# Six gate projections as three pairs of seven block products in a hybrid decoder block on one core

## The chip, the core and the metric

The kernel runs on one core of a Trainium2 chip. A core has a matrix engine (TensorE, PE in the tables, with its weight loads shown as PEld), a vector engine (VectorE, DVE), a scalar engine (ScalarE, ACT), GpSimd (POOL) and a queue that issues transfers (SyncE, SP). Each engine works off its own list of instructions in order and waits where an operand is not there yet. The metric is the device time of one execution in microseconds (us).

## What is computed

One layer of a decoder block over 512 tokens of width 1024, behind 16 learned tokens. Two attention branches, each with a gate, are merged and projected:

```python
u = rmsnorm(h, pre_norm_g[l])
proj = u @ w_in[l]
(..., z_fox, gate_a, gate_b) = jnp.split(proj, split_idx, axis=-1)
y_mla = (o_mla * jax.nn.silu(z_mla)) @ w_br_mla[l]
y_fox = (o_fox * jax.nn.silu(z_fox)) @ w_br_fox[l]
mixed = (jax.nn.sigmoid(gate_a) * y_mla + jax.nn.sigmoid(gate_b) * y_fox) @ w_out[l]
h = h + rmsnorm(mixed, post_norm_g[l])
```

`gate_a` and `gate_b` are u times a 1024x1024 slice of `w_in` each. The kernel computes the sigmoid as a tanh. Branch 0 is the MLA branch (`gate_a`), branch 1 the FoX branch (`gate_b`).

## The kernel before

**Precision.** All large products are of fp32 accuracy out of three reduced ones: every operand is held as a high part and a remainder (h and l), and `hi*hi + hi*lo + lo*hi` is accumulated. A block of weights therefore passes ACT, which writes the high part (`nc.scalar.copy`, L130 or L1052), and then DVE, which subtracts it from the raw weights (`split_lo`, L103). PE starts a product with the high part; its third matmul is the first that needs the remainder.

**A direct unit** (`unit`, L175) makes 128 output features for 512 tokens: 8 contraction blocks times 3 passes, 24 matmuls with 512 columns. `gate_unit` (L526) is such a unit on u, named pg, and ends in a tanh on ACT into a tile th. A `py` unit (L1016) is one on the gated attention output. The list `gates` holds 16 gate units, eight of branch 1 and then eight of branch 0, in the order 0, 4, 1, 5, 2, 6, 3, 7.

**A pair** (`pair_py`, L1063) makes two feature blocks, i and i+4, of the FoX output at once. Tokens, contraction and features are halved, and seven block products (Strassen's scheme in Winograd's form) take the place of eight: each product has 4 contraction blocks times 3 passes, 12 matmuls with 256 columns. They accumulate in three tiles, x, z, y, in the order x, z, x, y, x, z, x. The sums of token blocks S1 to S4 are made once for all four pairs. The sums of weight blocks T1 to T4 are made anew for each pair on DVE (`comb`, L1061), and seven weight blocks are split on ACT and DVE (`take`, L1074). Two raw weight tiles (wraw) hold the blocks b11, b21 and b12, b22.

**Buffers.** The pool wp (L83) holds three raw tiles, three high and three low ones. A load, a cast or a split into one of them waits until its former reader is through.

**Order.** On PE the program's order holds (`manual_schedule`). On the other engines the framework places each instruction when its engine and operands are expected to be free, with the program's order as the priority. Loads go out on SP in the order that this gives.

**The merge stage.** Attention ends at about 402 us. In the order of PE, there follow the last gate units of branch 1 (two of them while the token sums are prepared on DVE), then four times a pair py and two gate units (the last of branch 1, and seven of branch 0), then the eight `py` units of branch 0 with the sixteenth gate unit behind the first of them, then the projection by `w_out`, which uses seven block products too. `halved_g(0)` (L1011) splits the MLA output for the `py` units. `tsum` (L1030) makes the weight sums of the last projection in the tiles tb, one step behind each of the pairs 1 and 2, two behind pair 3. `ssum` (L1037) makes its token sums, behind the `py` units 2, 6 and 7.

Of the kernel before, what the change touches and what calls it, by code (L numbers as in the profile page):

```python
# [11 lines left out]
F32 = mybir.dt.float32  # L12
# [11 lines left out]
S = 512  # L24
# [30 lines left out]
def block_kernel(ctx: ExitStack, tc: tile.TileContext, x, meta_tokens, pre_norm_g, w_in, fox_forget_b,  # L55
# [468 lines left out]
    thx = [None]  # L524

    def gate_unit():  # L526

        i, br = gates.pop(0)

        def done(_, ps):  # L530
            if len(ths) % 7 > 4:
                ths[i, br] = thx[0].tile([128, S], F32, tag="thx", name=f"th{i}{br}")
            else:
                ths[i, br] = thp.tile([128, L], F32, tag="th", name=f"th{i}{br}")[:, 0:S]
            nc.scalar.activation(ths[i, br], ps, AF.Tanh, scale=0.5)
        return unit(f"pg{i}{br}", win_w((O_GA, O_GB)[br], i), u_act, KD, REAL, done)

# [457 lines left out]
    with ExitStack() as mg:  # L995
# [8 lines left out]
        tb = [m1.tile([128, HK, 512], F32, tag=f"tb{n}", name=f"tb{n}") for n in range(4)]  # L1004
# [3 lines left out]
        sh, sl = ([t.rearrange("p k s -> p (k s)")[:, 1024 * j : 1024 * j + 1024].rearrange("p (k s) -> p k s", k=HK)  # L1008
                   for j in range(4)] for t in uT0)

        def halved_g(br):  # L1011
            for k in range(KD):
# [3 lines left out]
        def py(i, br):  # L1016
            def get():
                return by_k(wunit([wbr[br][:, :, 128 * i : 128 * i + 128]])[0], KD)

            def done(_, ps):  # L1020
                nc.vector.scalar_tensor_tensor(out=gT[br][:, i], in0=ths[i, br], scalar=1.0, in1=ps, op0=ALU.add, op1=ALU.mult)
# [29 lines left out]
        def split_to(to, src):  # L1051
            nc.scalar.copy(to[0], src)  # L1052
            split_lo(nc.vector, to[1], src, to[0])
# [6 lines left out]
        def comb(out, p, q, op=ALU.subtract):  # L1060
            nc.vector.tensor_tensor(out=out, in0=p, in1=q, op=op)  # L1061

        def pair_py(i, br):  # L1063

            j, g, wb = i + HK, gT[br], wbr[br]
            ra, rb = (wload([wb[:, :, 128 * f : 128 * f + 128]])[1] for f in (i, j))
            yield
            b11, b21, b12, b22 = ra[:, 0:512], ra[:, 512:], rb[:, 0:512], rb[:, 512:]
            X, Y, Z = (sp.tile([128, 512], F32, tag="s", name=f"{n}{i}{br}")[:, 0:256] for n in "xyz")
            c11, c21, c12, c22 = g[:, i, lo_], g[:, i, up], g[:, j, lo_], g[:, j, up]  # L1070
            th1, th2 = ths[i, br], ths[j, br]
            room = []

            def take(src):  # L1074
# [16 lines left out]
            def gated(dst, th, ts, ps, add):  # L1091
                if add:
                    nc.vector.tensor_tensor(out=dst, in0=ps, in1=dst, op=ALU.add)
                return nc.vector.scalar_tensor_tensor(out=dst, in0=th[:, ts], scalar=1.0, in1=dst if add else ps, op0=ALU.add, op1=ALU.mult)

            w11 = take(b11)
            comb(b11, b12, b11)
            t1 = take(b11)
# [1 line left out]
            comb(b12, b22, b12)  # L1100
            comb(b11, b22, b11)
            t2 = take(b11)
            prod(X, A11, w11, True, False)
            nc.scalar.copy(c11, X)
            w21 = take(b21)
            prod(Z, S1, t1, True, False)
            nc.scalar.copy(c22, Z)
            t3 = take(b12)
            comb(b21, b21, b11)
            prod(X, S2, t2, False, False)  # L1110
            nc.scalar.copy(c12, X)
            w22 = take(b22)
            prod(Y, A12, w21, True, True)
            gated(c11, th1, lo_, Y, True)
            t4 = take(b21)
            prod(X, S3, t3, False, False)
            gated(c22, th2, up, X, True)
            prod(Z, S4, w22, False, True)
            gated(c12, th2, lo_, Z, True)
            prod(X, A22, t4, False, True)  # L1120
            closed[i] = gated(c21, th1, up, X, False).ins

        closed = {}
        pairs = [pair_py(i, 1) for i in range(HK)]
        with tc.issue_after(normed[0]):
            split_to(A11, g11)
            split_to(A22, g22)
            comb(g22, g21, g22, ALU.add)
            split_to(S1, g22)
        run(gate_unit())  # L1130
        next(pairs[0])
        with tc.issue_after(normed[0]):
            comb(g21, g11, g21)
            comb(g11, g22, g11)
            split_to(S2, g11)
        next(pairs[0])
        run(gate_unit())
        with tc.issue_after(normed[0]):
            split_to(A12, g12)
            comb(g12, g12, g11)  # L1140
            split_to(S3, g21)
            split_to(S4, g12)
        for i in range(HK):
            for _ in pairs[i]:
                pass
            for half in range(2):
                run(gate_unit())
            if i == 0:
                for n, (q, c) in enumerate(((0, 0), (0, 1), (1, 1), (1, 0))):
                    for half in range(2):  # L1150
                        k0 = HK * q + 2 * half
                        nc.sync.dma_start(tb[n][:, 2 * half : 2 * half + 2], wout[:, k0 : k0 + 2, 512 * c : 512 * c + 512])
            with tc.issue_after(closed[i]):
                for n in ((), (0,), (1,), (2, 3))[i]:
                    for half in range(2):
                        tsum(n, half)
        halved_g(0)
        for n, i in enumerate(PAIRED):
            py(i, 0)
            if gates:  # L1160
                run(gate_unit())
            elif n >= 4:
                done = n // 2 if n < 7 else HK
                if n in (4, 5, 7):
                    ssum(slice({4: 0, 5: 2, 7: 3}[n], {4: 2, 5: 3, 7: 4}[n]))
# [149 lines left out]
```

## Time and profile before

| what | value |
|---|---|
| median of three runs | 594.4 us (593.88 to 594.96) |
| profiled execution, its own time | 594.59 us |
| its span, first to last instruction | 592.5 us |
| PE busy | 584.1 us, 99% of the span |
| PEld busy | 501.0 us, 85% |
| DVE busy | 412.3 us, 70% |
| ACT busy | 357.8 us, 60% |
| POOL busy | 200.3 us, 34%, nothing after 400 us |
| mean granted TensorE clock | 0.998 |

Matmuls are pipelined, so the mean duration of one matmul (about 390 ns with 512 columns) is longer than the step from one to the next. Steps are read from the chain of work, where 24 or 48 matmuls in a row stand with their time. The same holds to a smaller degree on DVE and ACT: rows of several instructions in sequence give the step. Starts are given in us from the span's start.

### The profile page before, as it was taken

Reading aid. Unit: us, or ns where it says so; the run is one execution under the profiler, and the core shown is the slowest. Engines: PE = TensorE matmul, PEld = TensorE weight load, DVE = VectorE, ACT = ScalarE, POOL = GpSimd, SP = SyncE. Lnnn points to the kernel's source line nnn. Section 1 sums busy time; section 2 is a strip of 40 time slices with the busy share of each in tenths; the row PEclk is TensorE's granted clock in tenths of the full one; section 3 lists DMA queues with packets and bytes.
Section 4 is the critical chain, followed back from the end, with each engine's and each line's share of the span. In section 5 each row is a group of like instructions: output and inputs, shape, how many; then the busy total and the mean of one; then the engine's idle time right before and its main releaser. Section 6 shows DMA issues by size and latency. Waiting matters only on the chain.

```text
span 592.5 us, 11129 instructions
## 1 busy us (share of the span) xinstructions
PE 584.1 (99%) x3841; PEld 501.0 (85%) x3841; DVE 412.3 (70%) x1155; ACT 357.8 (60%) x816; POOL 200.3 (34%) x271
## 2 busy tenths in 40 slices
PE   8999999999999999999999999999999999999996
PEld 6989789889889888888898897888998998888884
DVE  5854876775775776766758748797647777468957
ACT  7846775784774784766748748764444363433753
POOL 4317746455358463553544544420000000000000
PEclk9999999999999999999999999999999999999999
DMA  8535599999995998896895986866822534333603
GB/s 288 119 87 161 124 176 239 230 201 225 168 201 116 229 211 217 188 188 175 177 207 147 203 160 146 193 137 216 273 72 71 143 95 132 94 106 108 213 2 142
DMA packets 220001, 97.47 MB, mean 165 GB/s; under 512 B 131457, under 2 KB 209673, under 8 KB 219945
## 3 DMA queue, kind: packets, MB, share of 16 engines
q1 hardware_dynamic: 219944, 96.77, 69.4%
q8 instruction: 30, 0.49, 0.3%
q14 instruction: 27, 0.21, 0.1%
HBM read 62.36 MB, written 3.97 MB: 112 GB/s over the span
## 4 chain that ended last, share of the span: by engine, by line
PE 97%; DMA 1%; SPq 0%; DVE 0%; issue 0%; POOL 0%; DVEq 0%; ACT 0%; POOLq 0%
PE z L97 19%; PE pg L97 15%; PE v L97 9%; PE st L97 8%; PE fk L97 8%; PE fq L97 8%; PE x L97 8%; PE py L97 7%; PE ov L97 5%; PE psm L97 4%; PE y L97 2%; PE mq L97 2%; PE mk L97 1%; DMA wsr<-in_w_in_dram 1%; PE ppe L97 1%; PE pt L100 1%
## 5 line engine op out<-in xcount | busy, mean ns | idle before, releaser
L103 POOL TENSOR_TENSOR wl<-wraw,wh 128x1024 fp32r<-128x1024 f32 (+2 forms) x62 | 120.2, 1947 | 96.3 <-ACT wh L130 73.9
L130 ACT CAST wh<-wraw 128x1024 fp32r<-128x1024 f32 (+1 forms) x72 | 74.6, 1040 | 53.5 <-PE py L97 16.8
L791 ACT ACTIVATE sf<-sf,nb 128x272 f32<-128x272 f32 (+3 forms) x128 | 72.5, 568 | 17.1 <-DVE nb L783 15.6
L819 DVE SCALAR_TENSOR_TENSOR pn<-sf,ri,pn 128x128 f16<-128x128 f32 (+3 forms) x128 | 68.7, 576 | 7.3 <-ACT pn L818 7.1
L103 DVE TENSOR_TENSOR wl<-wraw,wh 128x512 fp32r<-128x512 f32 (+1 forms) x54 | 51.0, 947 | 27.5 <-ACT wh L1052 18.9
L818 ACT ACTIVATE pn<-sf,ri 128x128 f16<-128x128 f32 (+3 forms) x128 | 61.2, 550 | 9.9 <-ACT sf L791 7.9
L97 PE MATMUL z<-uTh,wh 128*128 128x512 f32 x128 | 51.0, 398 | 0.0
L97 PE MATMUL pg<-uTh,wh 128*128 128x512 f32 x128 | 50.3, 393 | 0.0
L97 PE MATMUL z<-uTl,wh 128*128 128x512 f32 x128 | 50.1, 391 | 0.0
L97 PE MATMUL z<-uTh,wl 128*128 128x512 f32 x128 | 50.0, 391 | 0.0
L97 PE MATMUL pg<-uTl,wh 128*128 128x512 f32 x128 | 49.9, 390 | 0.0
L97 PE MATMUL pg<-uTh,wl 128*128 128x512 f32 x128 | 49.9, 390 | 0.0
L97 PE MATMUL st<-hlk,hlq 64*128 64x272 f32 (+3 forms) x480 | 45.5, 308 | 0.0
L1052 ACT CAST wh<-wraw 128x512 fp32r<-128x512 f32 x28 | 17.3, 619 | 39.8 <-DVE wraw L1061 15.4
L687 DVE TENSOR_REDUCE vsc<-v 128x1 f32<-128x272 f32 (+1 forms) x32 | 13.2, 433 | 39.9 <-PE v L97 39.9
L97 PEld LDWEIGHTS st<-hlk,hlq 64*128 64x128 f32 x480 | 34.6, 185 | 6.0 <-ACT vh L706 2.8
L97 PE MATMUL v<-uTh,wl 128*128 128x256 f32 (+1 forms) x128 | 36.5, 285 | 0.0
L97 PE MATMUL fk<-uTl,wh 128*128 128x256 f32 (+1 forms) x128 | 36.5, 285 | 0.0
L97 PE MATMUL fk<-uTh,wh 128*128 128x256 f32 (+1 forms) x128 | 36.5, 285 | 0.0
L97 PE MATMUL v<-uTl,wh 128*128 128x256 f32 (+1 forms) x128 | 36.5, 285 | 0.0
L97 PE MATMUL fk<-uTh,wl 128*128 128x256 f32 (+1 forms) x128 | 36.4, 285 | 0.0
L97 PE MATMUL v<-uTh,wh 128*128 128x256 f32 (+1 forms) x128 | 36.4, 285 | 0.0
(285 smaller groups left out, 1615.4 us busy)
## 6 DMA issues: line engine op xcount, KB each, us to landing
wraw<-in_w_in_dram SPq DMA_DIRECT2D x56, 512.0 KB, 4.5
cbp<-c_dram SPq DMA_DIRECT2D x16, 264.0 KB, 4.5
wraw<-in_w_br_fox_dram SPq DMA_DIRECT2D x8, 512.0 KB, 4.4
tb<-in_w_out_dram SPq DMA_DIRECT2D x8, 512.0 KB, 5.2
wraw<-in_w_br_mla_dram SPq DMA_DIRECT2D x8, 512.0 KB, 4.1
wraw<-in_w_out_dram SPq DMA_DIRECT2D x6, 512.0 KB, 3.6
xr<-in_x_dram SPq DMA_DIRECT2D x4, 512.0 KB
out_dram<-yo SPq DMA_DIRECT2D x8, 256.0 KB, 2.0
```

Source lines behind the costliest of these rows:

```text
L97: nc.tensor.matmul(*a, **k)
L100: nc.tensor.transpose(*a)
L103: return eng.tensor_tensor(out=lo, in0=src, in1=f32(hi), op=ALU.subtract)
L130: nc.scalar.copy(wh[:, :n], raw[:, :n])
L687: nc.vector.tensor_reduce(out=sc[:, i : i + 1], in_=ps, op=ALU.max, axis=AX.X, apply_absolute_value=True)
L791: exps[g] = nc.scalar.activation(sf, sf, AF.Exp, bias=sums["nb"][:, h, b : b + 1], scale=-1.0, accum_out=sums["su"][:, h, b : b + 1]).ins
L818: normed[:] = [nc.scalar.activation(hi, sf, AF.Copy, scale=rib).ins]
L819: nc.vector.scalar_tensor_tensor(out=lo, in0=sf, scalar=rib, in1=hi, op0=ALU.mult, op1=ALU.subtract)
L1052: nc.scalar.copy(to[0], src)
```

## The change

Six of the eight gate units of branch 0, feature blocks 0, 4, 1, 5, 2, 6, become three pairs of seven block products. Blocks 3 and 7 stay direct units. `pair` is the old body of `pair_py` with the sources, the token blocks and the two endings (a first copy out of PSUM, the closing) as arguments; `pair_gate` calls it on u and closes with tanh in pieces of 256 tokens.

The token blocks are views of u. Their four sums and their splits (`sums_u`) are made once, on DVE and ACT, in new tiles s0 to s3 and with two scratch areas in gT1; u itself is only there as its two parts, so that each sum adds both.

The order is new: pair 0 of py, the eighth gate unit of branch 1, then py 1, pg 0, py 2, pg 1, py 3, pg 2, the loads and first splits of each pair placed ahead of the end of the one before (`advance`). The tiles tb and their eight loads come after the last gate pair, and `tsum` after the `py` units with n = 1, 2 and 3 of the last loop.

```diff
-    gates = [(i, br) for br in (1, 0) for i in PAIRED]
+    gates = [(i, 1) for i in PAIRED] + [(i, 0) for i in PAIRED[6:]]
...
-        def pair_py(i, br):
+        def pair(name, srcs, A, copied, closing):
+
+            ra, rb = (wload([src])[1] for src in srcs)
             yield
...
+            a11, a12, a22, s1, s2, s3, s4 = A
             w11 = take(b11)
             comb(b11, b12, b11)
             t1 = take(b11)
...
             t2 = take(b11)
+            yield
+            X, Z, Y = (sp.tile([128, 512], F32, tag="s", name=f"{n}{name}")[:, 0:256] for n in "xzy")
+            prod(X, a11, w11, True, False)
+            copied(0, 0, X)
...
+            prod(Z, s4, w22, False, True)
+            yield
+            closing(1, 0, Z, True)
+            prod(X, a22, t4, False, True)
+            closing(0, 1, X, False)
...
+            def closing(f, t, ps, add):
+                dst = th[f][:, tss[t]]
+                if add:
+                    nc.vector.tensor_tensor(out=dst, in0=ps, in1=dst, op=ALU.add)
+                nc.scalar.activation(dst, dst if add else ps, AF.Tanh, scale=0.5)
+            o = (O_GA, O_GB)[br]
+            return pair(f"pg{i}{br}", [win[:, :, o + 128 * f : o + 128 * f + 128] for f in fs], (*ublocks, *us), copied, closing)
...
+        def sums_u(part):
+
+            plus = lambda out, p, q: comb(out, p, q, ALU.add)
+            (h11, l11), (h21, l21), (h12, l12), (h22, l22) = ([f32(t) for t in hl] for hl in (u11, u21, u12, u22))
+            if part == 0:
+                plus(r1, h21, l21)
+                plus(r2, h22, l22)
+                plus(r2, r1, r2)
+                split_to(us[0], r2)
+            else:
+                comb(r1, h11, r1)
+                plus(r1, l11, r1)
+                comb(r2, r2, h11)
+                comb(r2, r2, l11)
+                split_to(us[1], r2)
+                split_to(us[2], r1)
+                comb(r2, h12, r2)
+                plus(r2, l12, r2)
+                split_to(us[3], r2)
...
+        held(sums_u, 0)
+        finish(pairs[0])
+        sums_u(1)
+        run(gate_unit())
+        queue = [g for i in range(1, HK) for g in (pairs[i], pair_gate(i - 1, 0))]
...
+        for n in range(len(queue)):
+            advance(n, 4)
+            if n + 1 < len(queue):
+                advance(n + 1, 3)
+            finish(queue[n])
+        with tc.issue_after(passed[0]):
+            halved_g(0)
+        suc.close()
...
+                nc.sync.dma_start(tb[n][:, 2 * half : 2 * half + 2], wout[:, k0 : k0 + 2, 512 * c : 512 * c + 512])
+        run(gate_unit())
         for n, i in enumerate(PAIRED):
             py(i, 0)
             if gates:
                 run(gate_unit())
-            elif n >= 4:
...
+            with tc.issue_after(closed[i]):
+                for m in {1: (0,), 2: (1,), 3: (2, 3)}.get(n, ()):
+                    for half in range(2):
+                        tsum(m, half)
+            if n in (4, 5, 7):
+                ssum(slice({4: 0, 5: 2, 7: 3}[n], {4: 2, 5: 3, 7: 4}[n]))
```

What this does to the order is seen best on DVE, at three places.

First, DVE between the last split of pair 0 (wl63) and the weight split of the eighth gate unit of branch 1 (wl64), before:

```order
L103 TENSOR_TENSOR wl62_5634<-wraw58_5543,wh62_5633 128x512 x2
L103 TENSOR_TENSOR wl63_5668<-wraw57_5541,wh63_5667 128x512
L1093 TENSOR_TENSOR gT1_779<-y01_5550,gT1_779 128x256
L1094 SCALAR_TENSOR_TENSOR gT1_779<-th01_949,gT1_779 128x256
L103 TENSOR_TENSOR wl64_5715<-wraw64_5712,wh64_5714 128x1024
```

and the same place after, from the first row behind wl63, where L1069 are the sums of u in gT1, s1l is a split of one of them, and L1138 and L1139 are the closings of pair 0:

```order
L1069 TENSOR_TENSOR gT1_779<-gT1_779,uTl_69 128x1024
L1138 TENSOR_TENSOR gT1_779<-ypy01_5616,gT1_779 128x256
L1138 TENSOR_TENSOR gT1_779<-xpy01_5614,gT1_779 128x256
L1139 SCALAR_TENSOR_TENSOR gT1_779<-th01_949,gT1_779 128x256
L1139 SCALAR_TENSOR_TENSOR gT1_779<-th41_5334,gT1_779 128x256
L103 TENSOR_TENSOR s1l_5503<-gT1_779,s1h_5502 128x1024
L1138 TENSOR_TENSOR gT1_779<-zpy01_5615,gT1_779 128x256
L1069 TENSOR_TENSOR gT1_779<-uTh_68,gT1_779 128x1024
L1139 SCALAR_TENSOR_TENSOR gT1_779<-th41_5334,gT1_779 128x256
L1139 SCALAR_TENSOR_TENSOR gT1_779<-th01_949,xpy01_5614 128x256
L1069 TENSOR_TENSOR gT1_779<-uTl_69,gT1_779 128x1024
L103 TENSOR_TENSOR wl64_5739<-wraw64_5736,wh64_5738 128x1024
```

The split wl64 moved from the third place behind wl63 to the twelfth. Eight more rows of the sums of u and their splits stand further ahead, between the splits of the token sums of py (a2l) and wl63.

Second, DVE inside a pair of the alternating part. Before, py 2 from its first weight sum (wraw74 from wraw75, T1) to the split of b12 and b22 (wl78):

```order
L1061 TENSOR_TENSOR wraw74_5981<-wraw75_5983,wraw74_5981 128x512
L1061 TENSOR_TENSOR wraw75_5983<-wraw75_5983 128x512
L103 TENSOR_TENSOR wl76_5989<-wraw74_5981,wh76_5988 128x512
L103 TENSOR_TENSOR wl77_5998<-wraw74_5981,wh77_5997 128x512
L1061 TENSOR_TENSOR wraw74_5981<-wraw75_5983,wraw74_5981 128x512
L1061 TENSOR_TENSOR wraw74_5981<-wraw74_5981 128x512
L103 TENSOR_TENSOR wl77_5998<-wraw74_5981,wh77_5997 128x512
L103 TENSOR_TENSOR wl78_6030<-wraw75_5983,wh78_6029 128x512 x2
```

After, the gate pair pg 1 from the same sum (wraw83 from wraw84) to the same split (wl87); th and gT1 rows are closings of py 2:

```order
L1069 TENSOR_TENSOR wraw83_6137<-wraw84_6139,wraw83_6137 128x512
L1139 SCALAR_TENSOR_TENSOR gT1_779<-th61_5546,gT1_779 128x256
L1069 TENSOR_TENSOR wraw84_6139<-wraw84_6139 128x512
L103 TENSOR_TENSOR wl85_6142<-wraw83_6137,wh85_6141 128x512
L1138 TENSOR_TENSOR gT1_779<-zpy21_6043,gT1_779 128x256
L1069 TENSOR_TENSOR wraw83_6137<-wraw84_6139,wraw83_6137 128x512
L1139 SCALAR_TENSOR_TENSOR gT1_779<-th61_5546,gT1_779 128x256
L1139 SCALAR_TENSOR_TENSOR gT1_779<-th21_5467,xpy21_6042 128x256
L103 TENSOR_TENSOR wl86_6151<-wraw83_6137,wh86_6150 128x512 x2
L103 TENSOR_TENSOR wl87_6203<-wraw84_6139,wh87_6202 128x512
L1069 TENSOR_TENSOR wraw83_6137<-wraw83_6137 128x512
L103 TENSOR_TENSOR wl87_6203<-wraw84_6139,wh87_6202 128x512
```

Four closings of the pair before moved in among the weight sums. With two raw tiles for each pair and three buffers, the tile of b12 and b22 (wraw72, 78, 84, 90, 96) takes the same buffer every time, so that the load for the next pair goes out when the two splits of this one (the last of these rows) are done.

Third, DVE around the closing of `py` unit 2 of branch 0 (L1021 on py200), before:

```order
L103 TENSOR_TENSOR wl97_6659<-wraw97_6656,wh97_6658 128x1024
L103 TENSOR_TENSOR a2l_5500<-gT0_778,a2h_5499 128x512
L1043 TENSOR_TENSOR gT0_778<-gT0_778 128x2x256 x2
L103 TENSOR_TENSOR uTl_69<-gT0_778,uTh_68 128x512
L1043 TENSOR_TENSOR gT0_778<-gT0_778 128x2x256
L1021 SCALAR_TENSOR_TENSOR gT0_778<-th20_6172,py200_6568 128x512
```

and after, from the row behind that closing, where L1051 are the token sums of the last projection, uTl their splits, and wl109 the weights of `py` unit 3 (wl97 before):

```order
L1051 TENSOR_TENSOR gT0_778<-gT0_778 128x2x256
L1033 TENSOR_TENSOR gT0_778<-gT0_778,gT1_779 128x512
L1051 TENSOR_TENSOR gT0_778<-gT0_778 128x2x256
L103 TENSOR_TENSOR a1l_5494<-gT0_778,a1h_5493 128x256
L1051 TENSOR_TENSOR gT0_778<-gT0_778 128x2x256
L103 TENSOR_TENSOR uTl_69<-gT0_778,uTh_68 128x512
L1051 TENSOR_TENSOR gT0_778<-gT0_778 128x2x256
L103 TENSOR_TENSOR uTl_69<-gT0_778,uTh_68 128x512 x2
L1028 SCALAR_TENSOR_TENSOR gT0_778<-th60_6441,py600_6836 128x512
L103 TENSOR_TENSOR uTl_69<-gT0_778,uTh_68 128x512
L1033 TENSOR_TENSOR gT0_778<-gT0_778,gT1_779 128x512
L103 TENSOR_TENSOR wl109_6880<-wraw109_6877,wh109_6879 128x1024
```

The weight split of `py` unit 3 stood ahead of the closing of unit 2; now it stands behind the closing of unit 6, which is the last unit before unit 3 on PE.

More of the change, by code (lines that the diff above doesn't have):

```diff
@@ L1003, in block_kernel @@
         sp = mgg.enter_context(tc.tile_pool(name="sp", bufs=5, space=PSUM))
-        tb = [m1.tile([128, HK, 512], F32, tag=f"tb{n}", name=f"tb{n}") for n in range(4)]
+        tb = []
         a1 = [m1.tile([128, HK, 256], F32R, tag=n, name=n) for n in ("a1h", "a1l")]
@@ L1119, in pair_py @@
[L1119 to L1123, printed above, removed]
-        pairs = [pair_py(i, 1) for i in range(HK)]
[L1125 to L1129, printed above, removed]
+            prod(X, s3, t3, False, False)
+            closing(1, 1, X, True)
+            prod(Z, s4, w22, False, True)
@@ L1130, in block_kernel, with finish, held @@
+        def finish(steps):
+            for _ in steps:
+                pass
+        def held(fn, *a):
+            with tc.issue_after(normed[0]):
+                fn(*a)
+        pairs = [pair_py(i, 1) for i in range(HK)]
+        held(split_to, A11, g11)
+        held(split_to, A22, g22)
+        held(comb, g22, g21, g22, ALU.add)
+        held(split_to, S1, g22)
         run(gate_unit())
         next(pairs[0])
[L1132 to L1135, printed above, removed]
+        held(comb, g21, g11, g21)
@@ L1136, in block_kernel @@
+        held(comb, g11, g22, g11)
+        held(split_to, S2, g11)
         next(pairs[0])
         run(gate_unit())
[L1138 to L1145, printed above, removed]
-            for half in range(2):
[L1147 to L1156, printed above, removed]
```

84 lines of the change are left out of this document (55 added, 29 removed).

## The prediction

> **What bounds the kernel now.** I read the busy times first, then the chain of work, then the stage on DVE.
>
> ```profile
> PE 584.1 (99%) x3841; PEld 501.0 (85%) x3841; DVE 412.3 (70%) x1155; ACT 357.8 (60%) x816; POOL 200.3 (34%) x271
> ```
>
> PE carries the span, and the chain of work from 415 us on never leaves it until the end:
>
> ```profile
> 415.56 1.43 PE x L97 x12
> 416.99 1.44 PE z L97 x12
> 418.43 1.38 PE x L97 x12
> 419.81 1.42 PE y L97 x12
> 421.23 1.38 PE x L97 x12
> 422.61 1.36 PE z L97 x12
> 423.97 1.61 PE x L97 x12
> 425.58 10.91 PE pg L97 x48
> 436.49 1.43 PE x L97 x12
> ...
> 488.32 10.91 PE pg L97 x48
> 499.22 5.44 PE py L97 x24
> 504.66 5.44 PE pg L97 x24
> 510.10 38.08 PE py L97 x168
> 548.18 5.49 PE x L97 x24
> ```
>
> The reader sees the prices on PE. Seven block products take 425.58 - 415.56 = 10.02 us; two direct units take 10.91 us, a step of 10.91/48 = 0.227 us. DVE in the same stage:
>
> ```profile
> 415.56:425.58 10.02, 10.02 (x85) 9.90 (x85) 6.16 (x11) 5.25 (x10) 0.00 (x0) 1.00 0.87 287
> 436.49:457.42 20.93, 20.93 (x134) 18.92 (x134) 14.69 (x22) 8.34 (x15) 0.00 (x0) 1.00 0.38 101
> 530.00:540.00 10.00, 10.00 (x46) 8.29 (x45) 9.93 (x16) 5.50 (x8) 0.00 (x0) 1.00 0.28 90
> ```
>
> Behind the length stand PE, PEld, DVE and ACT. A pair with two direct units leaves DVE 20.93 - 14.69 = 6.2 us free; at 530 to 540 us DVE has nothing free. So PE is the bound only because DVE is a little ahead. What DVE work costs:
>
> ```profile
> 405.73 1.23 DVE L103 TENSOR_TENSOR a1l<-gT,a1h 128x1024 fp32r<-128x1024 f32 x1 [1.24 <-ACT a1h L1052]
> 410.92 0.69 DVE L103 TENSOR_TENSOR wl<-wraw,wh 128x512 fp32r<-128x512 f32 x1 [0.45 <-ACT wh L1052]
> 411.92 0.69 DVE L103 TENSOR_TENSOR wl<-wraw,wh 128x512 fp32r<-128x512 f32 x1 [0.30 <-ACT wh L1052]
> ...
> 416.02 0.69 DVE L103 TENSOR_TENSOR wl<-wraw,wh 128x512 fp32r<-128x512 f32 x1 [2.69 <-ACT wh L1052]
> 417.02 0.69 DVE L103 TENSOR_TENSOR wl<-wraw,wh 128x512 fp32r<-128x512 f32 x1 [0.31 <-ACT wh L1052]
> 419.00 0.69 DVE L103 TENSOR_TENSOR wl<-wraw,wh 128x512 fp32r<-128x512 f32 x1 [1.28 <-ACT wh L1052]
> 421.27 0.42 DVE L1093 TENSOR_TENSOR gT<-y,gT 128x256 f32<-128x256 f32 x1 [1.58 <-PE y L97]
> ...
> 422.27 1.23 DVE L103 TENSOR_TENSOR wl<-wraw,wh 128x1024 fp32r<-128x1024 f32 x1
> 423.42 0.42 DVE L1093 TENSOR_TENSOR gT<-x,gT 128x256 f32<-128x256 f32 x1
> 423.87 0.42 DVE L1094 SCALAR_TENSOR_TENSOR gT<-th,gT 128x256 f32<-128x256 f32 x1
> ...
> 489.22 4.62 DVE L1035 TENSOR_TENSOR tb<-tb,tb 128x1024 f32<-128x1024 f32 x4
> 493.75 2.49 DVE L103 TENSOR_TENSOR gl<-gT,gh 128x512 fp32r<-128x512 f32 x4
> ```
>
> In brackets stands the idle time ahead of a row and what ended it. In sequence a row of 1024 elements costs 1.15 us (four in 4.62), one of 512 costs 0.62 (four in 2.49), one of 256 about 0.40.
>
> **The change, part by part.**
>
> *a. Fewer matmuls.* Three gate pairs of 10.02 us for three times 10.91: -2.7 us. [...]
>
> *b. The eighth gate unit of branch 1.* Its weights' remainder (wl64) is now behind the sums of u on DVE. From a1l at 405.73 to wl64, the order holds 17 rows of 1024, 6 of 512 and 7 of 256: 17 x 1.15 + 6 x 0.62 + 7 x 0.40 = 26.1 us, so wl64 is done at 431.8; before, it was done at 423.5. PE ends pair 0 at 425.58 at the earliest, does two matmuls with the high part (0.45 us) and stands. The other 22 take 22 x 0.227 = 5.0 us, to 436.8, where 425.58 + 5.45 = 431.0 was due: +5.8 us. A wait inside the 26.1 us would lengthen it; starting some rows earlier would shorten it, but the row at 405.73 is itself released by ACT. Bounds 5.0 and 6.5.
>
> *c. The alternating part.* The load of b12 and b22 for the next pair goes out once this pair's splits of them are done. The transfers:
>
> ```profile
> wraw<-in_w_in_dram SPq DMA_DIRECT2D x10, 512.0 KB, 4.0
> tb<-in_w_out_dram SPq DMA_DIRECT2D x8, 512.0 KB, 5.2
> ...
> DMA to landing us min/median/max: 3.6/4.1/4.6
> ```
>
> The last line is of all raw weights from 380 to 520 us. The loop from one T1 to the next is this DVE work and one load. In a py pair it is 9 rows of 512 and one of 256, 6.0 us; in a gate pair 9 and 4, 7.2 us; with 4.1 and 0.1 for the issue, 10.2 and 11.3, together 21.5 us against 20.0 on PE. From 436.8 on: pair py 1 is undisturbed (to 446.8); T1 of pg 0 comes behind py 1's fifth product, at 444.2 (436.8, five products of 7.0 in all, and its add of 0.4); then 455.5, 465.7, 477.0, and 487.2 for pg 2. Its third product needs the split of T2, 5.3 us behind T1 (6 rows of 512, 4 of 256), at 492.5. From there PE needs 10 matmuls (1.15 us) and four products (5.8 us): 499.5, where 436.8 + 6 x 10.02 = 496.9 was due: +2.6 us. With 3.6 us per load it is +0.6, with 4.6 us +4.6; never below 0, since PE needs its 10.02 each.
>
> *d. Gate unit 3 behind pg 2.* The eight splits of the MLA output now stand ahead of its weights. On ACT:
>
> ```profile
> 487.61 2.18 ACT L1013 CAST gh<-gT 128x512 fp32r<-128x512 f32 x4
> 489.70 1.04 ACT L130 CAST wh<-wraw 128x1024 fp32r<-128x1024 f32 x1
> ```
>
> DVE begins behind the first of these casts, at 495.6 (the copy of pg 2's third product, at 493.7, then a cast of 0.6, the copy and the first gh). It has 8 x 0.62 + 3 x 0.40 + 1.15 = 7.3 us to wl101, at 502.9. PE could use it at 499.5 + 0.45: +2.9 us. Bounds 1 and 4: ACT may give the casts sooner or later.
>
> *e. `py` unit 3.* Its split wl109 is now behind the closing of unit 6, and DVE has the eight tsum rows (8 x 1.15 = 9.2 us) in the units ahead. Counted from E, the end of unit 4 on PE: behind unit 5 (E + 10.88) DVE has 3 rows of 512 and 4 of 1024, to E + 17.3; then 12 of 512, one of 256 and wl109, 9.0 us, to E + 26.3. PE wants it at E + 4 x 5.44 + 0.45 = E + 22.2: +4.1 us. If DVE only waits for the closing of unit 6 it is 2.6; with waits for ACT in between 5.5.
>
> *f. At nothing.* Two covers:
>
> ```profile
> 410.79 0.59 ACT L535 ACTIVATE th<-pg 128x512 f32<-128x512 f32 x1
> ...
> 417.03 0.37 ACT L1104 COPY gT<-x 128x256 f32<-128x256 f32 x1
> ...
> L1152 SPq DMA_DIRECT2D tb<-in_w_out_dram x8: 368/508/756, 404.5 to 412.3; - x8
> ```
>
> ACT gets per pair seven casts of 0.6, three copies of 0.37 and four short tanh of some 0.4 instead of two casts of 1.04 and two tanh of 0.59: about 4 us more in 20.9, where it had 20.93 - 8.34 = 12.6 us free; if that is gone, it lengthens c. The tb loads, now issued when pg 2 is nearly done, lie ahead of the raw weights of `py` unit 4 (wraw104) in SP's queue. Before, the first was issued at 404.5 and the last landed at 412.3 + 5.2, 13 us in all; PE reaches unit 4 some 19 us behind pg 2 (units 3, py 0 and 7 with the wait in d). If that cover failed, some 2 us. The part behind 548.18 is as it was.
>
> Sum: -2.7 + 5.8 + 2.6 + 2.9 + 4.1 = +12.7 us on the profiled execution's 594.59 us (0.2 above the median): **607.3 us**.
>
> **The rivals.**
>
> *The clock falls in the stalls.* The end of the trace shows that it can:
>
> ```profile
> 1.45 4.64 PE L97 MATMUL spun<-KPL 128*128 128x512 f32 x10 [1.45 <-DVE KPL L231]
> ...
> 586.00:592.50 6.50, 0.69 (x4) 0.22 (x2) 3.54 (x6) 0.98 (x3) 0.00 (x0) 0.85 0.45 173
> ```
>
> PE's last matmul is at 586.7, and the mean clock of the window is 0.85; at half rate that is the last 2 us, some 3.8 us behind the last matmul. The stall in b lasts 5.4 us. Ten matmuls of 512 columns take 4.64 us at the start, 2.4 us more than at 0.227; the recorded clock is 1.00 there, so that the cause isn't shown, but it bounds a cold start. One such start: 609.7 us; two (b and e): 612.1. [...]
>
> *The loop of c is longer than counted.* Each hand-over between ACT and DVE shows gaps of 0.3 to 2.7 us in the rows above, and I counted none within the loop. Half a microsecond more per operation that waits (three per pair) gives 1.5 us for five pairs: 615 us.
>
> *Other side: no stall.* If wl64 is done before 426.0, that is, if DVE has 5.8 us less ahead of it, and the rest follows, only a remains: 594.59 - 2.7 = 591.9 us. For it: DVE stood idle 6.6 us between 405.73 and wl64 before. Against it: those 6.6 us are already used up in the count, and the order puts twelve new rows (13.8 us) ahead.
>
> *Gain and stalls cancel.* For 594.6 us, c and d would have to vanish, b be 2 us and e 0.7; no row speaks for it. That the products aren't replaced is excluded: the order of PE holds them.
>
> **How the numbers follow.** Forecast 0.45, falling clock 0.30, longer loop 0.17, no stall 0.04, cancelling 0.04. Low ends: -2.7 + 5.0 + 0.6 + 1 + 2.6 = +6.5, 601 us; high ends -2.7 + 6.5 + 4.6 + 4 + 5.5 = +17.9, 612.5; with the clock 615. Runs differ by 0.2%, about 1.2 us, so this is what can be told from no change. Half of the cancelling case counts as same: faster 0.04, same 0.02, slower 0.94.
>
> **What would show it.** a: x, z and y on tiles pg of about 10 us per pair. b: PE idle before pg in 425 to 432, released by DVE wl. c: DVE rows T1 waiting for wraw, pairs of 10.4 to 11 us. d and e: PE waits of about 3 and 4 us for DVE wl, the second between two py units near 550. I am wrong if DVE is idle while PE waits in b or e, or if the clock falls.

## The result, and the profile after

The changed kernel takes **609.23 us** (median of six runs, 607.97 to 612.73), the kernel before 594.61 (six runs, 593.86 to 594.96): a ratio of 1.026, with a 95% interval of 1.0242 to 1.0278. The forecast was 607.3 us, 601 to 615. The profiled execution, on which the readings below rest, is the shortest of the six: 607.97 us, span 605.9.

The busy times and the granted clock in 40 slices, from the page of the changed kernel:

```profile
PE 586.4 (97%) x3949; PEld 504.8 (83%) x3949; DVE 441.4 (73%) x1204; ACT 370.2 (61%) x850; POOL 200.9 (33%) x271
...
PEclk9999999999999999999999999999899999998999
```

DVE has 29 us more work than before over the whole span; in the stretch that the change touches it has 117.1 instead of 91.7 us. These are the windows of both kernels from the first product of pair 0 to the last projection (in each: length, busy time of PE, PEld, DVE, ACT and POOL with instruction counts, clock, DMA share, GB/s), the kernel before first:

```profile
415.40:548.10 132.70, 132.70 (x746) 116.35 (x745) 91.65 (x136) 56.35 (x92) 0.00 (x0) 1.00 0.41 120
```

```profile
415.60:561.50 145.90, 135.08 (x854) 120.91 (x853) 117.09 (x183) 67.60 (x125) 0.00 (x0) 0.98 0.42 126
```

PE had no microsecond free there before; now it stands for 10.8 us. What it waited for, from the waits of PE between 415 and 606 us in the changed kernel (us in total, times, longest):

```profile
PE pg L97 <- DVE wl L103: 5.2, 2, 4.0
PE py L97 <- DVE wl L103: 3.9, 1, 3.9
PE pg L97 <- ACT wh L130: 0.9, 1, 0.9
PE xpy L97 <- ACT gT L1133: 0.5, 1, 0.5
```

And the chain of work at the places that the prediction spoke of (start, us, what):

```profile
428.83 1.14 DVE gT L1069
429.97 1.15 DVE wl L103
431.16 6.81 PE pg L97 x22
...
452.28 3.64 DMA wraw<-in_w_br_fox_dram
456.01 0.71 DVE wraw L1069
...
462.37 3.59 DMA wraw<-in_w_in_dram
...
500.29 1.23 DVE wl L103
501.56 5.27 PE pg L97 x22
...
548.06 1.15 DVE wl L103
549.25 12.31 PE py L97 x46
```

At 429.97 stands wl64, behind a row of the sums of u (L1069 on gT); at 548.06 stands wl109. Between them stands wl101, at 500.29, and ahead of that the chain runs through one load and one T1 per pair. Three rows say more than the waits: 22 matmuls take 6.81 us at 431.16 and 5.27 us at 501.56, and 46 take 12.31 us at 549.25, where 46 x 0.227 = 10.4. At the first and the last of these places the granted clock has fallen, to 0.50 behind 431 us, after it stood at 1.00 while PE waited. Windows of the changed kernel:

```profile
427.00:431.00 4.00, 0.12 (x1) 0.00 (x0) 4.00 (x6) 1.24 (x2) 0.00 (x0) 1.00 0.00 0
431.00:434.40 3.40, 3.24 (x8) 2.57 (x9) 3.40 (x6) 0.67 (x2) 0.00 (x0) 0.50 0.61 153
...
549.00:553.00 4.00, 3.75 (x11) 3.01 (x12) 4.00 (x8) 0.63 (x2) 0.00 (x0) 0.68 0.54 142
```

The ledger, from the starts of the matmuls on PE in the two profiled executions (us):

| stretch on PE | before | after | difference |
|---|---|---|---|
| start of pair 0 | 415.39 | 415.44 | +0.1 |
| pair 0 | 10.03 | 11.05 | +1.0 |
| eighth gate unit of branch 1 | 5.47 | 11.32 | +5.9 |
| py 1 to 3 with six gate blocks | 62.73 | 60.98 | -1.8 |
| gate unit 3, with the wait ahead | 5.44 | 7.88 | +2.4 |
| py 0 and gate unit 7 | 10.88 | 10.88 | 0 |
| `py` units 4, 1, 5, 2, 6, 3, 7 | 38.08 | 43.85 | +5.8 |
| last projection to the end of the span | 44.48 | 44.50 | 0 |

They sum to +13.4, the difference of the spans.

### The profile page after: what moved, and what is told of

It reads as the page before. It is cut to its first block, busy times and chain, and to the rows that moved or that the text cites. A ratio compares the mean times of both kernels' runs of the same rounds, so it can differ in the third digit from the quotient of the medians.

```text
span 605.9 us, 11431 instructions
## 1 busy us (share of the span) xinstructions
PE 586.4 (97%) x3949; PEld 504.8 (83%) x3949; DVE 441.4 (73%) x1204; ACT 370.2 (61%) x850; POOL 200.9 (33%) x271
## 4 chain that ended last, share of the span: by engine, by line
PE 83%; DVE 9%; DMA 3%; ACT 1%; issue 1%; SPq 1%; POOL 0%; DVEq 0%; ACTq 0%; POOLq 0%
PE z L97 17%; PE pg L97 9%; PE v L97 9%; PE st L97 8%; PE fk L97 8%; PE fq L97 7%; PE py L97 6%; PE ov L97 5%; PE x L97 4%; PE psm L97 3%; DVE wl L103 3%; DVE wraw L1069 2%; PE mq L97 2%; PE mk L97 1%; DMA wraw<-in_w_in_dram 1%; DMA wraw<-in_w_br_fox_dram 1%
## 5 line engine op out<-in xcount | busy, mean ns | idle before, releaser
L130 ACT CAST wh<-wraw 128x1024 fp32r<-128x1024 f32 (+1 forms) x66 | 68.1, 1039 | 32.0 <-PE py L97 13.9
L103 DVE TENSOR_TENSOR wl<-wraw,wh 128x512 fp32r<-128x512 f32 (+1 forms) x69 | 56.9, 842 | 8.4 <-ACT wh L130 4.7
L1060 ACT CAST wh<-wraw 128x512 fp32r<-128x512 f32 x49 | 29.4, 620 | 37.3 <-DVE wraw L1069 25.7
L692 DVE TENSOR_REDUCE vsc<-v 128x1 f32<-128x272 f32 (+1 forms) x32 | 13.2, 433 | 40.0 <-PE v L97 40.0
L97 PE MATMUL pg<-uTh,wl 128*128 128x512 f32 x80 | 32.3, 404 | 5.2 <-DVE wl L103 5.2
L97 PE MATMUL pg<-uTh,wh 128*128 128x512 f32 x80 | 32.3, 404 | 0.9 <-ACT wh L130 0.9
L97 PE MATMUL ov<-pt,vp 128*64 128x512 f16 (+4 forms) x416 | 32.6, 307 | 0.0
```

The lines of the kernel that those rows point to most:

```text
L97: nc.tensor.matmul(*a, **k)
L103: return eng.tensor_tensor(out=lo, in0=src, in1=f32(hi), op=ALU.subtract)
L130: nc.scalar.copy(wh[:, :n], raw[:, :n])
L692: nc.vector.tensor_reduce(out=sc[:, i : i + 1], in_=ps, op=ALU.max, axis=AX.X, apply_absolute_value=True)
```

## The experiments

The letters a to f are those of the prediction. The theory: the three waits b, d and e are a matter of the order on DVE; c is the loop through one load; the slow matmuls are a lowered clock behind a wait. The main rival: DVE has too much work in this stage, and a wait taken away at one place comes back at the next. Beside it: the matmuls are slow for another reason. Differences are to the changed kernel's 609.2 us, which was measured apart from these runs; the kernel before ran on the same chip as each group, at 594.1 to 594.5 us, where it had 594.6 beside the changed kernel.

**The sums of u later (e1).** Only their program place changes; the framework still put two of the four splits ahead of wl64.

```diff
-        sums_u(1)
         run(gate_unit())
...
             advance(n, 4)
+            if n == 0:
+                sums_u(1)
             if n + 1 < len(queue):
                 advance(n + 1, 3)
```

> Only the place of the second part of the sums of u changes: it stands in the program behind the eighth gate unit of branch 1 and behind the weight splits of py 1, so that wl64 needs fewer rows of DVE ahead of it (two of the sums' splits still come before it). If DVE's rows ahead of wl64 make the stall of 4.0 us, it shrinks to 0 to 2 us and what remains of the sums goes into py 1 and pg 0, where DVE has some 6 us free per pair, so that the time falls by 2 to 4 us; if the stall also costs the clock (22 matmuls in 6.81 us where 5.0 are due), by 1.8 us more: 604 to 606 us in all. Rival, the work on DVE is only put off: the same 4 us of waiting turn up before the products of py 1 or pg 0, and the time stays at 609 us within 1 us.

Measured 605.28 us (ratio to before 1.0182, 1.0166 to 1.0197), 3.9 less. The chain of this kernel:

```profile
426.72 5.48 PE pg L97 x24
...
545.69 13.47 PE py L97 x46
```

b is gone whole: 24 matmuls in 5.48 us. Of its 5.9 us, 2.1 came back in the six pairs (63.1 instead of 61.0 us), so that both are right in part: the wait is the order's, but the put-off rows need DVE later. Another 1.2 us stand in e, where the 46 matmuls now take 13.47 us. They are not DVE's: PE waits 3.9 us there as before, and the half clock behind the wait lasts 6.8 instead of 3.4 us.

**Gate unit 3's weights first (e2).**

```diff
+        g3 = gate_unit()
+        g3[0][1].prep()
         with tc.issue_after(passed[0]):
             halved_g(0)
...
-        run(gate_unit())
+        run(g3)
```

> Gate unit 3's weights are loaded and split ahead of the splits of the MLA output. If term d is these eight splits ahead of wl101, PE's waits at 499.7 (0.9 for ACT wh and 1.1 for DVE wl, and some slow matmuls) go: 606.6 us, 2.6 less than the changed kernel. Rival, the wait only moves to py 0, which needs the splits of the MLA output: 609 us, no change.

Measured 606.35 us (1.0201, 1.0186 to 1.0216), 2.9 less, and the unit, 2.4 us shorter, takes its 24 matmuls in one piece, with no wait at py 0 behind it:

```profile
500.30 5.47 PE pg L97 x24
505.77 5.44 PE py L97 x24
```

d is the eight splits ahead of wl101.

**`py` 3's weights first (e3), and the transfers behind them (e5).** e3 casts and splits the weights of the units 6 and 3 ahead of the first token sums. (For this `py` is divided into `py_unit`, which makes a unit, and a step that runs it; these lines are not shown.)

```diff
+            if n == 4:
+                for f in PAIRED[5:7]:
+                    ready[f] = py_unit(f, 0)
+                    ready[f][0][1].prep()
             if n in (4, 5, 7):
                 ssum(
```

> The weights of py 6 and py 3 are cast and split ahead of the first token sums of the last projection, so that wl109 no longer stands behind the closing of unit 6. If term e is that order on DVE, PE's wait of 3.9 us before py 3 goes, and if the wait also lowered the clock (46 matmuls in 12.3 us where 10.4 are due), 1.9 us with it: 603.4 us; without the clock 605.3 us. Rival, DVE is simply full there and the wait turns up at py 7 or at the first product of the last projection: 608 to 609 us.

Measured 609.07 us (1.0249, 1.0234 to 1.0264): no gain. The chain shows the seven `py` units without a wait, and the loss behind them:

```profile
519.23 38.09 PE py L97 x168
559.14 0.50 SPq L1272
559.75 8.19 DMA wraw<-in_w_out_dram
...
570.38 3.94 PE y L97 x10
```

The waits of SP's queue name what held it:

```profile
SPq L1270 <- PE py L97: 5.0, 1, 5.0
```

The transfer of gp needs room that PE's last py unit frees, and in the new order the next three weight loads of the projection stand behind it on SP. e5 keeps the edit and moves the code of those transfers (gp and xr) behind that product:

```diff
-        nc.sync.dma_start(gp, post_norm_g[0:1].broadcast_to([128, D]))
...
         product(Y, a2, 0, lambda c: plain(1, 0, c), True, True)
+        nc.sync.dma_start(gp, post_norm_g[0:1].broadcast_to([128, D]))
```

> As e3_py3_first, and the transfers of gp and xr, which waited 5.0 us in SP's queue for PE's last py unit with two weight loads behind them, stand behind the second product of the last projection. If that queue is where the 5.8 us of term e went in e3_py3_first, they now come out: 603.4 us (609.2 - 5.8). Rival, DVE or the raw buffers are full there and the weights of that product are late all the same: 607 to 609 us.

Measured 603.42 us (1.0150, 1.0134 to 1.0165): 5.8 less, as worked out. e is the order on DVE, wait and slow matmuls together. So e3's time was the rival's, but not its reason: DVE keeps up with PE in e5, and the price in e3 was paid on SP's queue.

**PE kept busy (e4, e12).** e4 adds dummy matmuls ahead of the two long waits: `spin(n)` makes n matmuls of 512 columns on the tile uTh, their results unused.

```diff
         sums_u(1)
+        spin(18)
         run(gate_unit())
...
         for n, i in enumerate(PAIRED):
+            if n == 6:
+                spin(17)
             py(i, 0)
```

> 35 matmuls on old operands are added, 18 ahead of the eighth gate unit and 17 ahead of py 3, into a tile that nobody reads (work that the kernel does not need): they fill the two long waits, which stay. If an idle PE lowers the clock for the matmuls behind it, the 22 matmuls behind wl64 take 5.0 instead of 6.8 us and the 46 behind wl109 10.4 instead of 12.3: 605.5 us, and the runs scatter less than the 4.8 us of the changed kernel. If the slow matmuls have another cause (late operands, the weight loads), they stay slow: 609 us or, with the added work, up to 610.

Measured 614.34 us (1.0327, 1.0310 to 1.0345), 5.1 more. The chain and the waits of PE:

```profile
427.41 4.11 PE spin L97 x18
431.52 5.68 PE pg L97 x24
...
501.08 6.89 PE pg L97 x22
...
552.90 5.68 PE spin L97 x17
558.58 10.92 PE py L97 x48
```

```profile
PE spin L97 <- ACT uTh L1053: 6.8, 1, 6.8
```

At the first place it is as the clock theory says: the granted clock stays at 1.00, and 24 matmuls take 5.68 us. At the second the choice of operands was bad: uTh is being overwritten with the token sums there, and the dummies themselves waited 6.8 us. They then ran slow (17 in 5.68 us, 3.9 at the full step), and the 48 matmuls behind them ran at full speed (10.92). And the half clock came at a place where it hadn't been, gate unit 3 (6.89 us), behind the same two waits of 0.9 and 1.1 us as in the changed kernel; the last section takes that up. e12 has the second part alone, on the attention output:

```diff
         for n, i in enumerate(PAIRED):
+            if n == 6:
+                t = acc("spin")
+                for _ in range(17):
+                    mm(t, gh[:, 0, 0:128], gh[:, 0, :], start=True, stop=True)
             py(i, 0)
```

> The changed kernel with 17 matmuls on the attention output (results unused, work that the kernel does not need) ahead of py 3, where PE waits 3.9 us for wl109; unlike in e4_keep_busy their operands are there. The wait stays filled. If the idle time lowers the clock for the matmuls behind it, the 46 matmuls take 10.4 instead of 12.3 us: 609.2 - 1.9 = 607.3 us. If they are slow for another reason, they stay at 12.3 us and the time at 609 us or a little above.

Measured 607.95 us (1.0235, 1.0219 to 1.0251), 1.3 less. The interval overlaps that of the changed kernel, so that the time alone shows no gain; the trace does. The chain, and the window over the two units behind the dummies:

```profile
545.87 3.85 PE spin L97 x17
...
550.21 10.76 PE py L97 x46
```

```profile
549.60:561.00 11.40, 11.37 (x50) 9.08 (x49) 8.87 (x16) 3.24 (x8) 0.00 (x0) 1.00 0.54 174
```

With PE busy the clock stays at 1.00, and the same 46 matmuls take 10.76 instead of 12.31 us. Their operands, their weight loads and their order are the same here; what differs is that PE was busy ahead of them.

**The sums on GpSimd (e6).**

```diff
         def sums_u(part):
+            def comb(out, p, q, op=ALU.subtract):
+                nc.gpsimd.tensor_tensor(out=out, in0=p, in1=q, op=op)
```

> The nine sums of u are made on GpSimd, which does nothing behind 400 us; their splits stay on ACT and DVE. If b is the number of rows on DVE ahead of wl64 (nine rows of 1.15 us fewer, 10.4 us), the wait of 4.0 us and the slow matmuls behind it go, and nothing of it turns up in py 1: 609.2 - 5.8 = 603.4 us, 2 us less than e1_sums_later. Rival: GpSimd's rows are long (3.4 us where the profile before has pairs of them) and chained, so that the splits come late in DVE's queue, ahead of weights that PE wants: 606 to 612 us.

Measured 622.44 us (1.0465, 1.0435 to 1.0494), 13.2 more, beyond the rival's range. The timelines of POOL, DVE and PE in this kernel (start, duration, engine and line, operation, idle time ahead of it and its releaser):

```profile
408.51 3.49 POOL L1172 TENSOR_TENSOR gT<-uTh,uTl 128x1024 f32<-128x1024 f32 x1 [14.68 <-DVE a2l L103]
...
420.99 3.22 POOL L1172 TENSOR_TENSOR gT<-uTl,gT 128x1024 f32<-128x1024 f32 x1
```

```profile
409.61 3.47 DVE L103 TENSOR_TENSOR a2l<-gT,a2h 128x1024 fp32r<-128x1024 f32 x1
...
419.57 2.42 DVE L103 TENSOR_TENSOR s0l<-gT,s0h 128x1024 fp32r<-128x1024 f32 x1 [5.89 <-ACT s0h L1060]
421.91 2.85 DVE L103 TENSOR_TENSOR wl<-wraw,wh 128x512 fp32r<-128x512 f32 x1
```

```profile
432.66 0.58 PE L97 MATMUL xpy<-a1h,wh 128*128 128x256 f32 x1 [13.91 <-ACT gT L1133]
```

Two things: a row takes 2.4 to 3.5 us on POOL, and the rows of DVE shown here beside POOL's are long too (the one of 1024 elements at 409.61 takes 3.47 us, 1.15 otherwise, that of 512 at 421.91 takes 2.85, 0.62 otherwise). And DVE stood 5.9 us for the cast of s0h, and ACT, in order, 4.2 and 5.0 us for POOL's sums ahead of the casts of s2h and s1h, with the copy of pair 0's first product queued behind them, for which PE waited 13.9 us.

**The loop of c: the order of the loads (e7), T4's place (e9).** e7 loads b12 and b22 first:

```diff
-            ra, rb = (wload([src])[1] for src in srcs)
+            rb, ra = (wload([src])[1] for src in srcs[::-1])
```

> The two raw weight tiles of a pair are loaded in the other order, b12 and b22 first. The three raw buffers go round, so that the late load (now of b11 and b21) takes the buffer that the split of b22 frees, not the one that the split of T4, some 1.4 us later, frees. If the loop of c closes over that last split, each of the five pairs behind py 1 loses up to 0.5 us of waiting: 607.2 us, and T1's waits of 0.4 to 0.8 us for wraw go. Rival, the split of b11 is now as late as T1 was: 609.2 us within 1 us.

Measured 616.34 us (1.0366, 1.0343 to 1.0388), 7.1 more. The late load is now that of b11, and T1, which overwrites b11, has to wait for the cast and split of b11 behind the load. From the chain of this kernel: the late loads start 11.6 and 11.3 us apart, where the first two intervals were 10.1 and 10.6 in the changed kernel:

```profile
463.83 3.58 DMA wraw<-in_w_in_dram
467.50 0.63 ACT wh L1060
...
475.42 3.68 DMA wraw<-in_w_br_fox_dram
...
486.74 3.57 DMA wraw<-in_w_in_dram
```

Both theories fall: the wait didn't stay as long, it grew. That the loop closes over the load is confirmed, since one cast and one split more in it lengthen every pair: the six take 66.1 us instead of 61.0. Beside it the clock counts: it is at half speed for four pieces of 3.4 us here and for two in the changed kernel. e9 leaves the loads and writes T4 elsewhere:

```diff
-            comb(b21, b21, b11)
+            comb(b12, b21, b11)
...
-            t4 = take(b21)
+            t4 = take(b12)
```

> One change in the pair: T4 is written over b12 instead of b21 (loads in their old order). The tile of b11 and b21, whose buffer the next pair's b12 and b22 get, is then free behind the subtraction that makes T4, and not behind T4's cast and split, some 1.3 us later. If the loop of c closes over that last split, it falls from 10.4 to some 9.1 us, under PE's 9.8, and the five pairs behind py 1 take 9.8 each: 609.2 - 2.0 = 607.2 us, T1 no longer waits for wraw. Rival: the loop closes over something else, as e7_load_order may suggest, or DVE's rows come in another order and lengthen it: 609 to 612 us.

Measured 609.77 us (1.0259, 1.0243 to 1.0274): no gain. T4 now overwrites T3 and so stands behind T3's split in DVE's order; the loads still start 10.4 to 10.8 us apart, and PE waited 1.3 us in pair 0 for a copy of ACT. The trace of the changed kernel says why nothing was to be gained. Pair pg 0 on the chain, and then the cast of T4, which T4's split needs, on ACT:

```profile
450.96 0.69 DVE wraw L1069
451.65 0.61 DVE wl L103
452.28 3.64 DMA wraw<-in_w_br_fox_dram
```

```profile
451.74 0.62 ACT L1060 CAST wh<-wraw 128x512 fp32r<-128x512 f32 x1 [0.71 <-DVE wraw L1069]
```

The row at 450.96 makes T4, and the split behind it is that of b22, as in pg 1, whose order is shown with the change (wl87 from wraw84). The load, that of b12 and b22 for py 2, goes out as b22's split ends, at 452.28, before the cast of T4 is through, at 452.36. So T4's split never stood in the loop, and the premise of e7 and e9 was wrong. What can be said of c is that it is a loop of one load (3.6 us) and some 6.4 us of rows on DVE and casts on ACT, from T1 at 456.01 to the next load at 462.37.

**Together (e8, e10, e11).** e8 is e1, e2, e5 and e7.

> The four changes of order together: sums of u later, gate unit 3's weights first, py 3's weights first with the transfers behind, and b12 with b22 loaded first. If they add up: 609.2 - 3.9 - 2.9 - 5.8 - 2.0 = 594.6 us, and without any wait of PE for DVE over 1 us; the floor is 594.6 - 3.3 = 591.3 us, the kernel before less what three gate pairs save. Rival, a shared DVE load: what one order frees the next one takes, 598 to 601 us.

Measured 602.45 us (1.0130, 1.0114 to 1.0145); e7's edit, which alone cost 7.1, is part of it. e10 has e9's edit instead.

> The sums of u later, gate unit 3's weights first, py 3's weights first with the transfers behind, and T4 in b12, with the loads in their old order. From e8_all_orders, less what the other order of loads cost alone (7.1 us) and less the loop of c (2.0 us): 602.4 - 7.1 - 2.0 = 593.3 us, beside 594.5 us of the kernel before: faster by 0.2%, at best 591.3 us. Rival, the put-off sums and the loop take the same DVE: 595 to 597 us, still slower than before.

Measured 595.61 us (1.0026, 1.0015 to 1.0036): 13.6 less than the changed kernel, and still 0.3% slower than the one before. The first row of PE's waits; the four behind it are of 0.2 us each:

```profile
PE xpy L97 <- ACT gT L1138: 1.3, 1, 1.3
```

The 1.3 us stand in pair 0, whose copy has the cast of s2h ahead of it on ACT; the pairs take 10.1 to 10.4 us. e11 takes up both: s2h behind the copies, and two transfers of half the size for b12 and b22.

```diff
-            ra, rb = (wload([src])[1] for src in srcs)
+            ra, rb = (wload(part)[1] for part in ([srcs[0]], [srcs[1][:, 0:HK], srcs[1][:, HK:KD]]))
...
-                split_to(us[2], r1)
+                with tc.issue_after(copies[2]):
+                    split_to(us[2], r1)
```

> e10_four_orders with two more changes: the cast and split of the third sum of u stand behind pair 0's third copy on ACT (they stood ahead of its first one, and PE waited 1.3 us for that copy), and b12 and b22 are loaded by two transfers of 256 KB instead of one of 512 KB, so that T1 waits for the first alone. The first gives 1.3 us. The load in the loop of c takes 3.5 us now; if it is half as long for half the bytes, the pairs lose their 0.5 us each (2.2 us in all), if it is mostly latency, nothing. In all 595.6 - 1.3 - 1.1 = 593.2 us (591.9 to 594.3), that is faster than the kernel before by 0.2%. Rival: the two puts-off fill DVE later (the wait for the copy turns up in py 1 or pg 0): 595.6 us.

Measured 595.68 us (1.0021, 1.0012 to 1.0030): the rival's number. The profile shows both edits at work, and the rest back at the next place. From the chain and the windows:

```profile
457.98 2.90 DMA wraw<-in_w_in_dram
```

```profile
415.60:548.00 132.40, 130.62 (x854) 118.74 (x853) 113.82 (x182) 68.39 (x126) 0.00 (x0) 1.00 0.44 132
```

The load takes 2.90 instead of 3.5 us, and py 3 and pg 2 take 9.84 and 9.76 us, so that c is gone there. But pair 0 still takes 11.04 us (10.03 before), py 1, pg 0 and py 2 take 10.74, 10.28 and 10.48, and the first two products of the last projection 0.9 us more than before. PE's matmuls from pair 0 to the last projection are 2.1 us shorter than before (130.62 for 132.70), and the waits that are left, 1.8 us, take up nearly all of it.

## Why the prediction was right, point by point

The time was right, the sign and the places of the waits too. The sum was 12.7 us; 13.4 were measured between the two profiled executions, and 14.6 between the medians. That the sum lies so near is in part luck, as the terms show:

| term | forecast | measured | of it matmuls behind a fallen clock |
|---|---|---|---|
| a and c, six pairs | -0.1 (-2.7 + 2.6) | -1.8 | 0 |
| b, with pair 0 | +5.8 | +6.9 | 1.8 |
| d | +2.9 | +2.4 | 0 |
| e | +4.1 | +5.8 | 1.9 |

The last column is what these matmuls took beyond 0.227 us each. Of the 1.8 and 1.9 us, 1.6 and 1.7 are the half clock itself (half of PE's busy time in the two stretches at 0.50); the other 0.2 are not explained, but a like amount stands behind the waits in gate unit 3, at full clock (22 in 5.27 instead of 5.0 us).

*a* was too small. A pair with a pair behind it takes 9.76 us (pg 0 of the changed kernel), its last product 1.42 instead of 1.53 us where direct units stood behind it; 10.91 - 9.76 is 1.15 us per pair, not 0.9 (2.7/3). The measured steps are 0.227 us with 512 columns (10.91/48) and 0.116 with 256 (9.76/84). The three py pairs, which now have a pair behind them too, gain some 0.2 us each.

*b.* The mechanism was right, and e1 shows it. wl64 was done at 431.1 us where 431.8 was forecast, so the wait was 0.7 us less than the count of rows said; PE began py 1 at 437.81 instead of 436.8, since the clock took 1.8. A part of it, not named in the prediction, is pair 0: three of its products started late behind ACT and DVE (1.0 us), hidden in the same wait.

*c.* With undisturbed pairs of 9.8 us, six take 58.8; they took 61.0, so c is 2.2 us. The size was right to half a microsecond, and the mechanism too: the load goes out as the split of b22 ends (452.28 us in pg 0, see e9). The loop was a little shorter than counted, 10.1 to 10.5 us from T1 to T1 where 10.2 and 11.3 were added up, with loads of 3.5 to 3.8 us instead of 4.1.

*d* and *e* are as forecast, d 0.5 us smaller, and the wait of e 3.9 instead of 4.1 us. e2 and e5 take them away whole. The cover named at *f* held: nothing waited for the tb loads. The covers of *f* did not include what ACT's casts of the sums do to pair 0's copies, 0.5 us here and 1.3 us in e9 and e10.

*The rivals.* The falling clock, to which a chance of 0.30 and 2.4 us per stall (the author's estimate, from the first ten matmuls) were given, was not an alternative to the forecast: it came on top, twice, with 1.8 and 1.9 us. It is also one of the signs by which the prediction said that it would be wrong. The forecast was near because a and c came out 1.7 us lower, and the waits of b, d and e together 1.4 us, which paid for 3.1 of the 3.7 us; that the two nearly cancel is luck. So the step that failed is that one: the forecast left the clock out of its sum. Without the slow matmuls the profiled execution would have been at some 604.3 us, an estimate. And this execution is the shortest of the six, with the highest mean clock (0.994, down to 0.986 in the longest), so that the median holds more of the clock still. The longer loop and the cases without a stall did not occur.

The experiments add what the prediction did not ask: with the three orders mended (e10, with T4 moved besides, and e11) the kernel is at 595.6 us, 0.2 to 0.3% slower than before. So the orders cost 13.6 of the 14.6 us, the clock that fell behind their waits included: in e10 and e11 it doesn't fall. The rest fits the rival that was set against the theory here: DVE's work in the stage grew by 25 us (22 in e11), and in e1 and e11 a part of the wait that was taken away shows up at the next place; in e2 and e5 it doesn't. That no order could be faster than before is not shown; the floor, if every wait went, would be an estimated 4 us below the kernel before (three pairs of 1.15 us and three of 0.2).

## What to carry to other kernels

To replace matmuls by sums of their operands, count the rows of the engine that makes the sums and splits between two dates that PE sets; here some 4 us of matmuls saved stood against 25 us of DVE rows in a stage where DVE had 41 us free, and where these rows stood made 13.6 of the 14.6 us that were lost. An instruction that is moved forward has to be followed on every queue that it passes: the gain of e3 was lost on SP, and 1.3 us of that of e10 on ACT. And where a wait of PE of about 4 us is forecast, the slow matmuls behind it belong in the sum: here they cost 1.8 to 3.1 us more than at the full step.

## What the runs showed of the hardware

*In these runs the half clock came in whole pieces of 3.4 us.* The stretches in which the granted clock was 0.5, from windows of 0.2 us over the same stage (each length is twice the clock that was lacking, summed over the windows):

| kernel | from (us), length (us) |
|---|---|
| before, e8, e10, e11 | none |
| changed | 430.8, 3.42; 550.4, 3.42 |
| e1 | 544.8, 6.82 |
| e2 | 429.2, 6.83; 548.6, 3.41 |
| e3 | 429.8, 6.83; 569.8, 3.41 |
| e4 | 501.4, 3.42; 549.2, 6.83 |
| e5 | 429.4, 6.83 |
| e6 | 421.2, 17.07; 561.2, 6.83 |
| e7 | 432.2, 3.42; 507.2, 3.41; 555.0, 6.83 |
| e9 | 429.4, 6.83; 552.4, 3.42 |
| e12 | 429.6, 6.83 |

All are 1, 2 or 5 times 3.41 us. They didn't begin a fixed time after PE's last matmul: at the same wait of 4.0 us, PE's last matmul starting at 426.5 to 426.8 us, the fall is at 429.2 in e2 and at 430.8 in the changed kernel. Within one run the starts, too, lie whole multiples of 3.413 us apart, to the 0.2 us of the windows (3.413 is (550.46 - 430.99)/35, from the two falls of the changed kernel; 35 in the changed kernel and e2, 41 in e3 and e6, 14 in e4, 22 and 36 in e7, 36 in e9). A piece that PE stood through for half was enough in these runs, as the stage shows when it is divided along each run's own pieces, in steps of 3.413 us from its falls (PE stood: it had no matmul by the profile's times):

| kernel | piece (us) | PE stood (us) | clock in the next piece |
|---|---|---|---|
| changed | 427.58 to 430.99 | 3.41 | 0.50 |
| changed | 547.05 to 550.46 | 2.20 | 0.50 |
| e4 | 498.18 to 501.59 | 2.00 | 0.50 |
| e7 | 503.93 to 507.34 | 1.74 | 0.50 |
| e9 | 545.57 to 548.99 | 1.86 | 1.00 |
| changed | 499.26 to 502.67 | 1.57 | 1.00 |

Over all the kernels, PE stood 1.7 us or more in every piece of the stage ahead of a fall, and at most 1.9 in the pieces at full clock that had none behind them. The clock came back behind a piece at 0.50 in which PE stood at most 0.4 us, and stayed down where it stood 0.8 or more. So in these runs a wait's price hung on where the borders of the pieces fell. The two waits of 0.9 and 1.1 us in gate unit 3 lie in one piece in e4, and 22 matmuls take 6.89 us behind them; in the changed kernel a border, at 499.26, parts them, and the matmuls take 5.27. Behind the wait of 4.0 us the clock stayed down for one piece in the changed kernel (22 matmuls in 6.81 us) and for two in e2 (7.64). This fits that the runs of the changed kernel lie 4.8 us apart and those of the kernel before 1.1.

*In e6, rows of POOL and DVE took longer side by side.* DVE's rows of 512 and 1024 elements, 0.62 and 1.15 us in sequence, took up to 2.85 and 3.47 us while POOL worked on float32 rows, and POOL's rows took 2.40 us while DVE stood (416.06) and up to 3.49 while it worked (408.51).

*Half a load was not there in half the time.* 512 KB took 3.5 to 3.8 us in the loop of the changed kernel, 256 KB 2.9 us in e11. The first half's load ended at 460.88 us; by 460.80 the windows of 0.2 us show some 440 KB moved, more than the first half, so that the two were under way together; a half alone was not measured.
